# Sixteen-column offsets of TensorE operands: value weights moved, a copied operand dropped, dummy products put in front of long runs

## Chip, cores and metric

The kernel runs on one core of one Trainium2 chip. The metric is device time in microseconds (us) of one execution, the median of several. Engines are named as in the profile: PE is TensorE, DVE is VectorE, ACT is ScalarE, POOL is GpSimd, SP is the engine that issues most DMAs; PEld is the loading of PE's stationary operand.

## The reference

Two layers on 512 tokens of width 1024, in float32: first an HGRN2 mixer, then dilated attention, each followed by a gated feed-forward network (FFN). Only these parts matter here:

```python
def dilated_attention_mixer(u, cos, sin, w_in, w_out):
    proj = (u @ w_in).astype(jnp.float32).reshape(B, S, N_GROUPS, 3, ATT_HEADS, ATT_HEAD_DIM)
    ...
    for gi, (window, dilation) in enumerate(DILATED_GROUPS):
        q = apply_partial_rope(proj[:, :, gi, 0], cos, sin) * scale
        k = apply_partial_rope(proj[:, :, gi, 1], cos, sin)
        v = proj[:, :, gi, 2]
        o_g, lse_g = dilated_group_attention(q, k, v, window, dilation)
    ...

def swiglu_ffn(u, w_in, w_out):
    gate, up = jnp.split(u @ w_in, 2, axis=-1)
    return (jax.nn.silu(gate) * up) @ w_out
```

The FFN's inner width is 2816, that is 22 blocks of 128; attention has three groups of 8 heads of 128.

## The kernel before

**Products.** A float32 product is made of three products of the type float32r: each operand is cut into a high and a low part (`uh`, `ul` for the tokens, `hiq`, `loq` or `spare` for weights), and high by high, high by low and low by high are summed in a PSUM bank. A product (one `matmul`) has a stationary operand of 128 columns, which PE loads first, and a moving operand, here of 256 columns for nearly all that the change touches. The profile writes a product as `out<-moving,...` or `out<-stationary,...` with two tile names; which of the two moves is told below.

**Seven products for eight.** Where a block of weights is multiplied with all tokens, both are cut in quarters and the result is made from seven quarter products with sums of quarters (Strassen's scheme in Winograd's form). One quarter product is four slices of the contraction by three, so 12 products; a *group* below is such a run of 12 (for values, two groups of 12, one for each half of a PSUM bank).

**The FFN** (`seven_products`, products at line 964). Per inner block of 128 (called an iteration here) there are seven groups, 84 products: `B11` (tokens' first quarter), `T3`, `t2`, `B21`, `t1`, `T4`, `B22`. Layer 0 has 16 such iterations and layer 1 has 18; the first blocks of each layer (`PLAIN`) are done with products 512 columns wide at lines 577 to 579, just ahead. The moving operands are the tokens `uh`, `ul` and the sums of their quarters `th`, `tl`; stationary are the weights, in tiles that begin `R0` = 16 columns into their place. The weights of iteration i+1 are cut and summed by ACT, DVE and POOL while PE works on iteration i; the order of all this is written out by hand at the end of `seven_products`.

**The copied operand.** `B11` exists twice: as it lies, for the first iteration, and as a copy 144 columns further on (`uh[:, k, 144:400]`), for all later ones. `shift()` makes the copy once per layer, in place, in the middle of the first iteration: two casts on ACT for `uh`, two on DVE for `ul` (line 897).

**Attention's projections** (`products`, line 1982) are tasks of a planner (`Plan`): each task has an engine, a cost and its reads and writes; `run` tries several rules, keeps the order with the earliest end, and then writes the instructions in that order on every engine. Queries and keys of two groups are made by seven products (`sevens`): moving are the tokens (`apart`, `uh`, `th`, `tl`), stationary the weights, 16 columns into their place (`R0`). Queries and keys of the remaining group (`plain`) are 512 wide. Values of these two groups (`value_unit`) are made by seven products with the roles changed: here the weights move, `V0` = 32 columns into their place, and the tokens are stationary. One value unit has seven results of 24 products; the planner puts the four units into two long runs of two units (336 products) each. Softmax, rotary embedding and sums over values run between these, on the other engines and in short products on PE (lines 2248, 2273, 2321, 2342).

**Offsets.** All operand tiles begin in SBUF at a multiple of 128 bytes, 32 columns of four bytes. So the place of an operand's first column, in columns modulo 32, is 0 or 16 for everything here. Written as moving/stationary, the products of the kernel before are:

| products | moving/stationary | the two are |
|---|---|---|
| FFN, all groups but the copied `B11` | 0/16 | unequal |
| FFN, `B11` from the second iteration on (144 columns further) | 16/16 | equal |
| queries and keys by `sevens` | 0/16 | unequal |
| values (32 columns into their place) | 0/0 | equal |

Of the kernel before, what the change touches and what calls it, by code (L numbers as in the profile page):

```python
# [11 lines left out]
F32 = mybir.dt.float32  # L12
# [5 lines left out]
P = 128  # L18
# [15 lines left out]
MAGIC = 12582912.0  # L34
WHOLE = ("quarters", "half")

R0, V0 = 16, 32


class Stream:  # L40
# [100 lines left out]
class Plan:  # L141
# [3 lines left out]
    DRAIN = {"DVE": 0.12, "ACT": 0.12}  # L145

    def __init__(self):
        self.tasks, self.names, self.seq = [], {}, {}

    def add(self, eng, cost, fn=None, r=(), w=(), goal=None, late=None, urgent=False):  # L150

# [85 lines left out]
    def run(self):  # L237

        ts = self.tasks
        for t in ts:  # L240
            for d in t["deps"]:
                ts[d]["outs"].append(t["id"])
        due = [0.0] * len(ts)
        for t in reversed(ts):
            at = min([due[o] - self.after(t, ts[o]) for o in t["outs"]], default=1e9)
            if t["goal"] is not None:
                at = min(at, t["goal"] + t["cost"])
            due[t["id"]] = at - t["cost"]
        tries = (self.trial(due, *rule) for rule in itertools.product((1, 2, 3, 5), (0.1, 0.2, 0.3), (5.0, 8.0, 1e9), (0.3, 1.0)))
        end, done, start = min(tries, key=lambda r: r[0])  # L250
        for t in done:
            t["start"], t["due"] = start[t["id"]], due[t["id"]]
        for t in done:
            if t["fn"]:
                t["fn"](t["eng"])
        return done
# [36 lines left out]
def block_kernel(tc, x, c, positions, ada_w, ada_b, norm_g, hgrn_w_in, lower, hgrn_norm_g, hgrn_w_out,  # L293
# [8 lines left out]
    with ExitStack() as ctx:  # L302
# [579 lines left out]
        def seven_products(fs, mid, seeded, spare, th, tl):  # L882
# [5 lines left out]
            t_of = lambda i: [(th[:, i, k], tl[:, i, k]) for k in range(4)]  # L888
            B21, B22 = u_of(1, 0), u_of(1, 1)

            B11 = [u_of(0, 0), [(uh[:, k, 144:400], ul[:, k, 144:400]) for k in range(4)]]

            def shift():

                for a, b in ((112, 256), (0, 112)):
                    for copy, t in ((act.copy, uh), (dve.tensor_copy, ul)):
                        copy(t[:, 0:4, a + 144:b + 144], t[:, 0:4, a:b].bitcast(F32))
            t1, T3, T4, t2 = (t_of(i) for i in range(4))

            W = shared.rearrange("p a (b n) -> p (a b) n", b=2)  # L900
# [74 lines left out]
            with tc.manual_schedule(engines=ORDERED):  # L975
# [10 lines left out]
                for i in range(len(fs)):  # L986
                    more = i + 1 < len(fs)
                    R, Sm = places(i)
                    s = Sums(i)
                    run(s.first, R, 0, B11[i > 0], True)  # L990
                    run(s.both, Sm, 1024, T3, True)
                    if before:
                        gate_of(i - 1, before)
                    act.copy(s.u2, s.first)
                    if more:
                        r_lo(i + 1)
                        sum_a(i + 1)
                    if before:
                        value_of(i - 1, before)
                    run(s.u2, Sm, 0, t2, False)  # L1000
                    run(s.first, R, 1024, B21, False)
                    act.copy(W[:, 4 + i % 2], s.both)
                    act.copy(s.u4, s.u2)
                    if i == 0:
                        shift()
                    run(s.u4, Sm, 512, t1, False)
                    run(s.u2, R, 512, T4, False)
                    if more:
                        sum_b(i + 1)
# [604 lines left out]
        for p in range(4):  # L1614
# [11 lines left out]
            for k in range(2):  # L1626
# [5 lines left out]
                if k == 1:  # L1632
                    for i in range(2):
                        n = fl.n + i
# [338 lines left out]
        def split_place(first):  # L1973
            return plan.place("hl", 3, lambda: st.part_tiles(first))

        def products(cost, dst, key, terms, begin, reads):


            def go():
                todo = [p for t in terms() for p in t]  # L1980
                for i, (x, y) in enumerate(todo):
                    pe.matmul(dst(), x, y, start=begin and i == 0, stop=i == len(todo) - 1, skip_group_check=True)  # L1982
            of_units.append(len(plan.tasks))
            PE(cost, go, reads, [key])

        triple = lambda xh, xl, yh, yl: ((xh, yh), (xh, yl), (xl, yh))
        a_of = lambda r, c: [[a[:, r * 4 + k, c * 256:c * 256 + 256] for a in apart] for k in range(4)]
# [117 lines left out]
        def plain(g, hd):  # L2105
# [16 lines left out]
            def both():  # L2122
# [4 lines left out]
                def one(i, t):  # L2127
                    b = mm_of()
                    for part in range(4):
                        def terms(part=part):  # L2130
                            for kt in (2 * part, 2 * part + 1):
                                w = slice((i * KT + kt) * P, (i * KT + kt + 1) * P)
                                yield triple(p.t[0][:, w], p.t[1][:, w], apart[0][:, kt], apart[1][:, kt])
                        products(6 * 0.2275, lambda: b.t, b(), terms, part == 0, [p("h", i), p("l", i)])
                    scale = SCALE if i == 0 else 1.0
                    for hf in range(2):
                        o = i * 64 + hf * 32
# [12 lines left out]
        def value_unit(i, hf):  # L2150
# [46 lines left out]
            def run(tag, tile, o, us):  # L2197
                b, p = mm_of(tag), ps[tile]
                for n in range(2):
                    def terms(n=n):  # L2200
                        for kt in range(4):
                            w = slice(o * 1024 + kt * 256, o * 1024 + (kt + 1) * 256)
                            yield triple(*us(kt, n), p.t[0][:, w], p.t[1][:, w])
                    products(12 * 0.1165, lambda n=n: b.t[:, n * 256:(n + 1) * 256], b(), terms, n == 0, [p("h", o), p("l", o)])
                return b

            def add_to(out, one, b, f):
# [293 lines left out]
```

## Time and profile before

| | us |
|---|---|
| median of 3 executions (lowest, highest) | 1506.12 (1504.59, 1506.7) |
| the profiled execution | 1504.35 |
| its span | 1502.6 |
| PE busy in it | 1476.8 |
| DVE, ACT, POOL busy | 1095.8, 797.2, 191.3 |

The span is the time between the first and the last instruction; the profiled execution took 1.75 us more than it. PE's clock was granted in full (0.997 on average). A row of the view of groups reads: line, engine, operation, `out<-in` by tile names, shapes, count | busy time, mean duration in ns | idle time just before. A row of the timeline reads: start in us from the span's start, duration, engine, line, operation, names, shapes, count [idle time before it and what ended it]. Products overlap in PE's pipeline, so the duration of one (276 to 287 ns here) is longer than the distance from its start to that of the next; the distance is found from two start times and the number of products between them, and it is what a product costs.

### The profile page before, as it was taken

To read this page: it belongs to the slowest core of one execution; us is meant where nothing else is said; L and a number is where in the kernel's file an instruction comes from. 1 tells how busy PE (TensorE), PEld (TensorE's weight loads), DVE (VectorE), ACT (ScalarE), POOL (GpSimd) and SP (SyncE) were. 2 spreads that over 40 slices of the span, in tenths; PEclk is the share of its full clock that TensorE was granted. 3 is DMA by queue.
4 is the path that set the end of the run, shared out by engine and by line. 5 is a ranking of instruction groups with operands and counts; after the bars stand their busy time and mean duration, and the time that the engine had idled before them with its cause. 6 is when DMAs were issued, how large, how long until landed. Compare 5 with 4: busy or idle time off the path is not lost. (4 is left out here: it accounts for less than half of the span.)

```text
span 1502.6 us, 25061 instructions
## 1 busy us (share of the span) xinstructions
PE 1476.8 (98%) x9823; PEld 1323.5 (88%) x9823; DVE 1095.8 (73%) x1800; ACT 797.2 (53%) x1474; POOL 191.3 (13%) x172
## 2 busy tenths in 40 slices
PE   8999999999999999999999999999989999999998
PEld 6777788888999988788999999999978899999886
DVE  4587678487688885777798877888666978887533
ACT  4433343373455542267647878477875555555231
POOL 1011011031111100131001010001012211110100
PEclk9999999999999999999999999999999999999999
DMA  9654555124233346634344442345243333333531
GB/s 308 183 170 140 183 169 169 57 79 146 85 113 113 113 161 211 220 117 143 113 120 144 109 136 73 118 131 147 89 134 119 104 94 113 113 113 141 197 111 56
DMA packets 210151, 201.09 MB, mean 134 GB/s; under 512 B 8248, under 2 KB 167920, under 8 KB 209776
## 3 DMA queue, kind: packets, MB, share of 16 engines
q1 hardware_dynamic: 207056, 192.71, 41.3%
q10 hardware_dynamic: 1952, 6.65, 1.2%
q8 instruction: 77, 1.26, 0.4%
q0 software_dynamic: 1024, 0.13, 0.2%
q14 instruction: 42, 0.34, 0.1%
HBM read 192.31 MB, written 5.31 MB: 132 GB/s over the span
## 5 line engine op out<-in xcount | busy, mean ns | idle before, releaser
L90 ACT CAST hi<-raw 128x2048 fp32r<-128x2048 f32 x43 | 82.1, 1909 | 144.3 <-DMA raw<-in_ffn_w_out_dram 74.9
L91 DVE TENSOR_TENSOR lo<-raw,hi 128x2048 fp32r<-128x2048 f32 x43 | 103.7, 2413 | 65.7 <-ACT hi L90 65.6
L577 PE MATMUL ps_mm<-uh,hi 128*128 128x512 f32 (+1 forms) x400 | 145.6, 364 | 0.0
L578 PE MATMUL ps_mm<-ul,hi 128*128 128x512 f32 (+1 forms) x400 | 144.5, 361 | 1.1 <-DVE ul L677 1.1
L579 PE MATMUL ps_mm<-uh,lo 128*128 128x512 f32 (+1 forms) x400 | 143.9, 360 | 0.0
L1982 PE MATMUL ps_mm<-apart,hiq 128*128 128x256 f32 (+1 forms) x608 | 142.0, 326 | 0.1
L1982 PEld LDWEIGHTS ps_mm<-apart,hiq 128*128 128x128 f32 x608 | 100.0, 189 | 8.4 <-ACT xs L2096 0.3
L1982 PE MATMUL ps_mm<-apart,loq 128*128 128x256 f32 (+1 forms) x304 | 97.4, 321 | 0.4 <-DVE loq L2118 0.4
L964 PE MATMUL ps_mm<-tl,hiq 128*128 128x256 f32 x340 | 94.0, 276 | 0.0
L964 PE MATMUL ps_mm<-th,hiq 128*128 128x256 f32 x340 | 94.0, 276 | 0.0
L964 PE MATMUL ps_mm<-th,loq 128*128 128x256 f32 x340 | 94.0, 276 | 0.0
L955 DVE TENSOR_TENSOR loq<-raw,hiq 128x1024 fp32r<-128x1024 f32 x68 | 80.3, 1221 | 18.6 <-ACT hiq L951 18.6
L577 PEld LDWEIGHTS ps_mm<-uh,hi 128*128 128x128 f32 x400 | 75.2, 188 | 18.2 <-issue 6.7
L578 PEld LDWEIGHTS ps_mm<-ul,hi 128*128 128x128 f32 x400 | 75.4, 189 | 12.3 <-DVE ul L677 1.5
L579 PEld LDWEIGHTS ps_mm<-uh,lo 128*128 128x128 f32 x400 | 75.1, 188 | 12.4 <-issue 1.1
L578 PE MATMUL ps_mm<-lo,oh 128*128 128x512 f32 x208 | 81.5, 392 | 2.4 <-DVE lo L91 2.4
L935 POOL TENSOR_TENSOR raw<-raw 128x512 f32<-128x512 f32 x34 | 44.8, 1318 | 303.1 <-DVE spare L931 138.5
L577 PE MATMUL ps_mm<-hi,oh 128*128 128x512 f32 x208 | 81.5, 392 | 0.0
L951 ACT CAST hiq<-raw 128x1024 fp32r<-128x1024 f32 x68 | 68.0, 1047 | 18.7 <-DVE raw L939 17.1
L1982 PE MATMUL ps_mm<-uh,hiq 128*128 128x256 f32 x256 | 71.9, 281 | 0.0
L1982 PE MATMUL ps_mm<-uh,loq 128*128 128x256 f32 x256 | 71.3, 279 | 0.0
L1982 PE MATMUL ps_mm<-ul,hiq 128*128 128x256 f32 x256 | 71.3, 278 | 0.0
(479 smaller groups left out, 4632.8 us busy)
## 6 DMA issues: line engine op xcount, KB each, us to landing
raw<-in_ada_w_dram SPq DMA_DIRECT2D x40, 1024.0 KB, 5.1
raw<-in_ffn_w_in_dram SPq DMA_DIRECT2D x136, 256.0 KB, 4.1
raw<-in_ffn_w_out_dram SPq DMA_DIRECT2D x22, 1024.0 KB, 5.1
raw<-in_attn_w_in_dram SPq DMA_DIRECT2D x64, 256.0 KB, 4.6
raw<-in_hgrn_w_in_dram SPq DMA_DIRECT2D x12, 1024.0 KB, 5.3
raw<-in_attn_w_in_dram SPq DMA_DIRECT2D x12, 1024.0 KB, 5.2
raw<-in_ffn_w_in_dram SPq DMA_DIRECT2D x10, 1024.0 KB, 6.5
raw<-in_attn_w_in_dram SPq DMA_DIRECT2D x16, 512.0 KB, 4.6
```

The costliest lines, as they stand in the source:

```text
L90: self.nc.scalar.copy(hi, t)
L91: self.nc.vector.tensor_sub(lo, t, hi.bitcast(F32))
L577: pe.matmul(ps, ah, bh, start=start, stop=False, skip_group_check=part)
L578: pe.matmul(ps, ah, bl, start=False, stop=False, skip_group_check=part)
L579: pe.matmul(ps, al, bh, start=False, stop=stop, skip_group_check=part)
L935: pool.tensor_add(r[:, 2], r[:, 2], r[:, 0])
L951: act.copy(hi, src)
L955: dve.tensor_sub(lo, src, hi.bitcast(F32))
L964: pe.matmul(ps, w[x][:, a], us[kt][y], start=begin and kt + m == 0, stop=kt == 3 and m == 2, skip_group_check=True)
L1982: pe.matmul(dst(), x, y, start=begin and i == 0, stop=i == len(todo) - 1, skip_group_check=True)
```

## The change

Four things are changed.

`V0` becomes 48, so the values' moving weights begin 16 columns further on: values are now 16/0, unequal.

The copied `B11` and `shift()` go: every iteration of the FFN uses the operand as it lies, 0/16.

In the first iteration of each layer's FFN, between `B11` and `T3`, three dummy products are issued. They have the first stationary weights and, moving, `uh[:, 0, 16:272]`, that is 16/16, equal. They write the PSUM bank that `T3` starts anew just behind, so nothing of them is kept.

The planner gets a set `asides`. After the order is chosen, it walks along PE's tasks; a stretch of tasks that all make 256-wide projections is one run. In it, it takes the first task that starts a value result; if 12 tasks or more stand from there to the end of the run, three dummy products are issued ahead of that task, with its first stationary operand and moving weights 16 columns off (48 + 16 = 64, so 0/0, equal). The dummies have no cost in the plan, and the order of the tasks is not touched.

```diff
-R0, V0 = 16, 32
+R0, V0 = 16, 48
...
+        narrow = []
+        for t in [t for t in done if t["eng"] == "PE"] + [{}]:
+            if t.get("narrow"):
+                narrow.append(t)
+                continue
+            first = next((k for k, u in enumerate(narrow) if u["aside"]), len(narrow))
+            if len(narrow) - first >= 12:
+                self.asides.add(narrow[first]["id"])
+            narrow = []
...
-            B11 = [u_of(0, 0), [(uh[:, k, 144:400], ul[:, k, 144:400]) for k in range(4)]]
-
-            def shift():
-
-                for a, b in ((112, 256), (0, 112)):
-                    for copy, t in ((act.copy, uh), (dve.tensor_copy, ul)):
-                        copy(t[:, 0:4, a + 144:b + 144], t[:, 0:4, a:b].bitcast(F32))
+            B11 = u_of(0, 0)
...
-                    run(s.first, R, 0, B11[i > 0], True)
+                    run(s.first, R, 0, B11, True)
+                    if i == 0:
+                        for _ in range(3):
+                            pe.matmul(s.both, R[0][:, 0:P], uh[:, 0, 16:272], start=True, stop=True, skip_group_check=True)
                     run(s.both, Sm, 1024, T3, True)
...
-                    if i == 0:
-                        shift()
...
-        def products(cost, dst, key, terms, begin, reads):
-
+        def products(cost, dst, key, terms, begin, reads, aside=None, narrow=True):
+            me = len(plan.tasks)
 
             def go():
                 todo = [p for t in terms() for p in t]
+                for _ in range(3 if me in plan.asides else 0):
+                    pe.matmul(dst(), todo[0][0], aside(), start=True, stop=True, skip_group_check=True)
                 for i, (x, y) in enumerate(todo):
                     pe.matmul(dst(), x, y, start=begin and i == 0, stop=i == len(todo) - 1, skip_group_check=True)
-            of_units.append(len(plan.tasks))
+            of_units.append(me)
             PE(cost, go, reads, [key])
+            plan.tasks[me].update(narrow=narrow, aside=begin and aside is not None)
...
-                    products(12 * 0.1165, lambda n=n: b.t[:, n * 256:(n + 1) * 256], b(), terms, n == 0, [p("h", o), p("l", o)])
+                    products(12 * 0.1165, lambda n=n: b.t[:, n * 256:(n + 1) * 256], b(), terms, n == 0, [p("h", o), p("l", o)],
+                             lambda: p.t[0][:, o * 1024 + 16:o * 1024 + 272])
```

In the built program PE has 12 products more, in four places of three, and its order is otherwise the same. The first place is layer 0 of the FFN; on PE the seam between `B11` and `T3` in the first iteration was

```order
L964 MATMUL ps_a_3368<-uh,spare_3081 128x256
L964 MATMUL ps_a_3368<-ul,spare_3081 128x256
L964 MATMUL ps_a_3368<-uh,spare_3082 128x256
L964 MATMUL ps_a_3370<-th_3084,hiq_3374 128x256
L964 MATMUL ps_a_3370<-tl_3085,hiq_3374 128x256
```

and is now

```order
L967 MATMUL ps_a_3368<-uh,spare_3081 128x256
L967 MATMUL ps_a_3368<-ul,spare_3081 128x256
L967 MATMUL ps_a_3368<-uh,spare_3082 128x256
L996 MATMUL ps_a_3370<-uh,spare_3081 128x256 x3
L967 MATMUL ps_a_3370<-th_3084,hiq_3374 128x256
L967 MATMUL ps_a_3370<-tl_3085,hiq_3374 128x256
```

so the three dummies stand alone between the two groups; layer 1 has the same seam. The other two places are the long value runs. The first of them begins on PE behind the scores of a head (`qk`, line 2256 of the changed kernel), where now stands

```order
L2256 MATMUL ps_a_6475<-qk_6471,qk_6467 128x256 x2
L1986 MATMUL ps_mm_6662<-hiq_6577,apart_6291 128x256 x3
L1988 MATMUL ps_mm_6662<-hiq_6577,apart_6291 128x256
L1988 MATMUL ps_mm_6662<-loq_6578,apart_6291 128x256
L1988 MATMUL ps_mm_6662<-hiq_6577,apart_6292 128x256
```

with the three dummies ahead of the run's first product. In the second long run they stand ahead of the second value result (`ps_a_9082`), since the first result's 12 opening products are divided from the rest by a head's scores and sums, and a run that begins in the middle of a result gets its dummies at the next one.

On DVE the two casts of `shift()` are gone in each layer, and the sums for the second iteration's weights (line 942) come one place earlier. It was

```order
L931 TENSOR_TENSOR loq_3391<-raw_3191,hiq_3390 128x1536
L1053 TENSOR_TENSOR mid_3074<-ps_mm_3312,sg_3362 128x512
L897 CAST ul<-ul 128x4x144
L1053 TENSOR_TENSOR mid_3074<-ps_mm_3337,sg_3363 128x512
L897 CAST ul<-ul 128x4x112
L939 TENSOR_TENSOR raw_3191<-raw_3191 128x1024
L943 TENSOR_TENSOR raw_3191<-raw_3191 128x512
```

and is now

```order
L934 TENSOR_TENSOR loq_3391<-raw_3191,hiq_3390 128x1536
L942 TENSOR_TENSOR raw_3191<-raw_3191 128x1024
L1057 TENSOR_TENSOR mid_3074<-ps_mm_3312,sg_3362 128x512
L946 TENSOR_TENSOR raw_3191<-raw_3191 128x512
L1057 TENSOR_TENSOR mid_3074<-ps_mm_3337,sg_3363 128x512
```

ACT loses its two casts per layer without any other move; POOL and the DMA queues keep their order.

More of the change, by code (lines that the diff above doesn't have):

```diff
@@ L147, in __init__ @@
     def __init__(self):
-        self.tasks, self.names, self.seq = [], {}, {}
+        self.tasks, self.names, self.seq, self.asides = [], {}, {}, set()
     def add(self, eng, cost, fn=None, r=(), w=(), goal=None, late=None, urgent=False):
@@ L2133, in terms @@
                                 yield triple(p.t[0][:, w], p.t[1][:, w], apart[0][:, kt], apart[1][:, kt])
-                        products(6 * 0.2275, lambda: b.t, b(), terms, part == 0, [p("h", i), p("l", i)])
+                        products(6 * 0.2275, lambda: b.t, b(), terms, part == 0, [p("h", i), p("l", i)], narrow=False)
                     scale = SCALE if i == 0 else 1.0
```

## Prediction, made before the changed kernel ran

> **What bounds the kernel now.** I read the page first: PE is the bound almost everywhere, at full clock.
>
> ```profile
> span 1502.6 us, 25061 instructions
> PE 1476.8 (98%) x9823; PEld 1323.5 (88%) x9823; DVE 1095.8 (73%) x1800; ACT 797.2 (53%) x1474; POOL 191.3 (13%) x172
> ...
> PEclk9999999999999999999999999999999999999999
> ```
>
> So a nanosecond per product counts, and I looked for products of one shape that cost different amounts. PE's timeline around the FFN of layer 0 (rows at the seams of groups; the last two are from layer 1):
>
> ```profile
> 384.72 0.39 PE L579 MATMUL ps_mm<-uh,lo 128*128 128x512 f32 x1
> 384.95 0.28 PE L964 MATMUL ps_a<-uh,spare 128*128 128x256 f32 x1
> 386.36 0.28 PE L964 MATMUL ps_a<-th,hiq 128*128 128x256 f32 x1
> ...
> 394.84 0.28 PE L964 MATMUL ps_b<-uh,hiq 128*128 128x256 f32 x1
> 395.20 0.28 PE L964 MATMUL ps_b<-uh,hiq 128*128 128x256 f32 x1
> 396.28 0.29 PE L964 MATMUL ps_b<-th,hiq 128*128 128x256 f32 x1
> 396.63 0.28 PE L964 MATMUL ps_b<-th,hiq 128*128 128x256 f32 x1
> 397.65 0.28 PE L964 MATMUL ps_mm<-th,hiq 128*128 128x256 f32 x1
> 404.45 0.28 PE L964 MATMUL ps_a<-uh,spare 128*128 128x256 f32 x1
> 405.88 0.29 PE L964 MATMUL ps_a<-th,hiq 128*128 128x256 f32 x1
> ...
> 529.25 0.28 PE L964 MATMUL ps_b<-uh,hiq 128*128 128x256 f32 x1
> ...
> 1213.31 0.28 PE L964 MATMUL ps_b<-uh,hiq 128*128 128x256 f32 x1
> 1366.92 0.28 PE L964 MATMUL ps_b<-uh,hiq 128*128 128x256 f32 x1
> ```
>
> From 386.36 to 394.84 stand 72 unequal products (moving/stationary 0/16): 8.48/72 = 117.8 ns each. The second iteration begins with 12 equal ones (16/16, the copied `B11`), 1.44 us or 120 ns each. Three more products (396.28 to 396.63, 117 ns) and then 60 unequal ones, 397.65 to 404.45, take 113.3 ns. So the unequal products have two speeds, 117.8 (*slow*) and 113.3 (*quick*), and what stood between them was a stretch of equal products. Each later iteration repeats it: 1.43 us for its 12 equal products (119), the rest quick; thirteen iterations take 529.25 - 404.45 = 124.80, 9.600 each. Groups in the first iteration and in a quick stretch of the second tell the speeds by duration too:
>
> ```profile
> L964 PE MATMUL ps_mm<-th,hiq 128*128 128x256 f32 x8 | 2.2, 281 | 0.0
> ...
> L964 PE MATMUL ps_mm<-th,hiq 128*128 128x256 f32 x12 | 3.3, 276 | 0.0
> ```
>
> Then attention: queries and keys (rows 1 to 6), the value runs (the others).
>
> ```profile
> 777.58 0.28 PE L1982 MATMUL ps_mm<-uh,hiq 128*128 128x256 f32 x1
> 784.64 0.39 PE L1982 MATMUL ps_mm<-apart,hiq 128*128 128x512 f32 x1
> 798.54 0.28 PE L1982 MATMUL ps_mm<-uh,hiq 128*128 128x256 f32 x1
> 807.02 0.27 PE L2248 MATMUL ps_a<-qk,qk 128*128 128x128 f32 x1
> 809.93 0.28 PE L1982 MATMUL ps_mm<-uh,hiq 128*128 128x256 f32 x1
> 818.09 0.27 PE L2321 MATMUL ps_a<-ident,h 128*128 128x128 f32 x1
> ...
> 733.35 0.47 PE L1982 MATMUL ps_mm<-hiq,apart 128*128 128x256 f32 x1
> 736.42 0.28 PE L1982 MATMUL ps_a<-hiq,uh 128*128 128x256 f32 x1
> 773.85 0.28 PE L1982 MATMUL ps_mm<-apart,hiq 128*128 128x256 f32 x1
> ...
> 940.97 0.28 PE L1982 MATMUL ps_a<-hiq,uh 128*128 128x256 f32 x1
> 975.15 0.28 PE L1982 MATMUL ps_mm<-hiq,apart 128*128 128x256 f32 x1
> ```
>
> 777.58 to 784.64 are 60 unequal products at 117.7, 798.54 to 807.02 another 72 at 117.8; behind a head's scores (line 2248), 809.93 to 818.09, 72 of the same kind at 113.3. Either speed lasts through seven groups and all their tiles: it is a state of PE that something else sets. The equal values are never quick: 736.42 to 773.85 are 312 products at 120.0, 940.97 to 975.15 are 288 at 118.7.
>
> **FFN.** If the three equal dummies set the quick state, and it lasts, an iteration costs 84 x 0.1133 = 9.52 instead of 9.60. The first iteration had 9.89; it now has 12 x 0.1178 + 3 x 0.120 + 72 x 0.1133 + 0.02 for settling = 9.95, so +0.06. The second goes from 9.61 to 9.52, the 14 behind it save 0.08 each: layer 0 gains 0.09 + 1.12 - 0.06 = 1.15. Layer 1 runs (1366.92 - 1213.31)/16 = 9.60 too, with 17 iterations behind its first: 1.36 - 0.06 = 1.30. Together **-2.45**.
>
> That three products do the work of twelve is not shown. What I have is the first three of the twelve, 394.84 to 395.20: 120 ns each, already the pace of the whole stretch, so they are in their own rhythm at once; and that the change of speed comes two or three products after the offset turns back. I take it that the turn from equal to unequal sets the state. If it does not, every unequal product of the FFN is slow, the rival below.
>
> **Values.** From 0/0 to 16/0, behind dummies of 0/0: the mirror image of the FFN, 16 columns displaced. No product 16/0 is in the trace. Its bounds are 113.3 and 120.0; I take 113.3, by the FFN's seam, the only equal-to-unequal turn there in which the moving operand's offset changes. The first run: 336 x 6.7 ns = 2.25, less 3 x 0.12 + 0.02 = 0.38: -1.87. The second, behind its dummies: 312 x 5.4 = 1.68 - 0.38 = -1.30. Together -3.17.
>
> Who comes late then is DVE, which prepares all weights (first row: a window with the busy time of PE, PEld, DVE, ACT and POOL in it, the clock, and the share and GB/s of DMA; then DVE's timeline, and a row of PE's waits: us, count, mean):
>
> ```profile
> 751.00:785.00 34.00, 34.00 (x286) 33.83 (x285) 31.10 (x46) 14.51 (x21) 0.58 (x1) 1.00 0.40 114
> ...
> 751.02 0.69 DVE L2224 SCALAR_TENSOR_TENSOR V<-V,ps_mm 128x512 f32<-128x512 f32 x1 [1.58 <-PE ps_mm L1982]
> 782.42 0.42 DVE L2091 TENSOR_TENSOR qk<-xs,ps_mm 128x256 f32<-128x256 f32 x1 [0.80 <-ACT xs L2096]
> 784.38 1.23 DVE L2118 TENSOR_TENSOR loq<-raw,hiq 128x1024 fp32r<-128x1024 f32 x1
> ...
> PE ps_mm L1982 <- DVE loq L2118: 0.4, 1, 0.4
> ```
>
> From 751.00 to 785.00 DVE is busy 31.10 of 34.00 us, and PE waits 0.4 for its cut at 784.38. At 751.02 PE is (751.02 - 733.35)/0.120 = 147 products into the run, so earlier by 147 x 6.7 ns - 0.38 = 0.60; DVE shifts with it, and another 0.80 can come out of its wait at 782.42 (for ACT, which waits for PE): 1.40 against PE's 1.87. I charge **+0.4**, with 0 to 1.3 as bounds. In the second run DVE waits for others, and I charge nothing.
>
> What the first run's end does to queries and keys behind it is open too. 773.85 to 807.02 holds 168 slow unequal products: quick, they give -0.76, but the scores at 807.02 came between slow and quick, and may then do the reverse to the 84 behind (+0.38). I take 0 of -0.8 to +0.4.
>
> **Copies.** The view of line 897:
>
> ```profile
> L897 DVE CAST ul<-ul x4: 394/427/875, 382.2 to 1204.9; 128x576 fp32r<-128x576 f32 x2, 128x448 fp32r<-128x448 f32 x2
> L897 ACT CAST uh<-uh x4: 567/622/677, 389.7 to 1208.8; 128x576 fp32r<-128x576 f32 x2, 128x448 fp32r<-128x448 f32 x2
> ```
>
> Eight casts, about 2.5 us on ACT and 2 on DVE, in the first iterations; nobody waits for them there, PE's 84 products run without a gap. Value: 0.
>
> **Sum.** -2.45 - 3.17 + 0.4 = -5.2 on the profiled execution's 1504.35, so 1499.1. The median of three, 1506.12, is 1.8 above it: **1500.9**.
>
> The Trainium skill speaks against all of it. Its page "TensorE: Matmul & The Clock Gate" (section "Back-to-back issue gap") gives a spacing from the moving width alone, 109.2 ns for 256 columns, and says under "Step-by-step: what each phase is for" that moving and stationary operands have independent read ports. By that, dummies are pure cost, an estimated 12 x 109.2 = 1.3 us. The trace disagrees: 113.3, 117.8 and 120.0 ns for one width.
>
> **Rivals.**
>
> *The quick state is not set by three, or does not last.* Each iteration of the FFN now needs the state from its layer's only dummies, where before it was renewed by 12 equal products every 9.6 us. Without it 84 x 0.1178 = 9.895: layer 0 loses 15 x 0.295 + 0.36 = 4.8, layer 1 17 x 0.295 + 0.36 = 5.4, together +10.2; with the values at -2.8 that is +7.4, 1513.5, and 1516 if these stay slow too. It decides as soon as the state is lost within the first two thirds of a layer. For it: an unequal stretch never ran quick for longer than 84 products. Against: no quick stretch in the FFN falls back, nor has it stalls that could disturb it. Chance 0.22.
>
> *The values do not become quick*, since 16/0 behaves otherwise or the scores ahead of the run win. Slow at 117.8 they save 336 x 2.2 + 312 x 0.9 ns = 1.02 and cost 0.72 of dummies: with the FFN -2.75, 1503.4. Chance 0.19.
>
> *Offsets do nothing*, and the speeds have another cause, such as which iteration it is. Then the trace's rows stay and 12 dummies at 0.113 are added: +1.4, 1507.5. Against it is the timing of the seams. Chance 0.06.
>
> **How the numbers follow.** The likeliest, 0.53, is 1500.9; its own range, with a wait of DVE from 0 to 1.3, queries and keys from -0.8 to +0.4 and the runs' scatter of 1 us, is 1499 to 1503. The range takes in the second and third rival and the nearest of the first's partial losses: 1498.5 to 1509. 0.2% is 3.0 us, about what a measurement of this kernel can tell from no change. Faster by more: the likeliest and a part of the second rival, 0.60. Within: most of the second and half of the third, 0.17. Slower: the first and the rest, 0.23.
>
> **What would show it.** In line 967's groups of the changed kernel: 281 ns only in the first 12 products of each layer, 276 after; iterations of 9.52. In line 1988's value groups: 276 instead of 282 to 288. PE's wait for DVE near 785 grown from 0.4 to about 1. If the first `T3` group behind the dummies still shows 281, the forecast is wrong by some 10 us; if a later iteration turns to 281, the state does not last.

## The result, and the profile after

| | before, us | changed, us | ratio (95% interval) |
|---|---|---|---|
| first comparison, medians of 15 and 15 executions | 1504.23 | 1499.83 (1493.97 to 1503.32) | 0.9968 (0.9957 to 0.9979) |
| the same kernel again, 17 and 6 executions | 1503.39 | 1498.41 (1495.14 to 1502.71) | 0.9957 (0.9941 to 0.9973) |

The change makes the kernel faster by 0.32%, 4.8 us of 1504 (3.2 to 6.5), and by 6.5 us (4.1 to 8.9) the second time. 1500.9 us and -5.2 were predicted. The profiled execution took 1503.32 us and is the slowest of its 15, so the span below differs from that before by 1.0 us only; what it lost is told at the end of this section.

The head of the page of the changed kernel (1502.6 us and 1476.8 us of PE before):

```profile
span 1501.6 us, 25079 instructions
PE 1472.6 (98%) x9835; PEld 1317.9 (88%) x9835; DVE 1091.9 (73%) x1796; ACT 793.4 (53%) x1470; POOL 191.8 (13%) x172
```

PE's timeline at the FFN of layer 0 (the last two rows are of layer 1):

```profile
384.45 0.28 PE L967 MATMUL ps_a<-uh,spare 128*128 128x256 f32 x1
385.86 0.52 PE L996 MATMUL ps_a<-uh,spare 128*128 128x256 f32 x3
386.22 0.29 PE L967 MATMUL ps_a<-th,hiq 128*128 128x256 f32 x1
386.93 0.28 PE L967 MATMUL ps_a<-th,hiq 128*128 128x256 f32 x1
394.41 0.28 PE L967 MATMUL ps_b<-uh,hiq 128*128 128x256 f32 x1
...
527.69 0.28 PE L967 MATMUL ps_b<-uh,hiq 128*128 128x256 f32 x1
...
1213.64 0.28 PE L967 MATMUL ps_b<-uh,hiq 128*128 128x256 f32 x1
1365.96 0.28 PE L967 MATMUL ps_b<-uh,hiq 128*128 128x256 f32 x1
```

The dummies of line 996 take 0.36 us. The six products behind them still settle (386.22 to 386.93, 118 ns each); from there 66 products reach 394.41 at 7.48/66 = 113.3 ns. The fourteen iterations from 394.41 to 527.69 take 133.28/14 = 9.520 us each, the sixteen of layer 1 152.32/16 = 9.520 too: no iteration falls back. The view of groups for the first iteration tells it by duration (mean ns behind the comma):

```profile
L967 PE MATMUL ps_mm<-th,hiq 128*128 128x256 f32 x8 | 2.2, 276 | 0.0
```

Those `ps_mm` products were at 281 before. The value runs, in PE's timeline:

```profile
731.93 0.28 PE L1988 MATMUL ps_mm<-hiq,apart 128*128 128x256 f32 x1
734.66 0.28 PE L1988 MATMUL ps_a<-hiq,uh 128*128 128x256 f32 x1
770.02 0.28 PE L1988 MATMUL ps_mm<-apart,hiq 128*128 128x256 f32 x1
...
944.68 0.28 PE L1988 MATMUL ps_mm<-hiq,apart 128*128 128x256 f32 x1
977.32 0.39 PE L1988 MATMUL ps_mm<-apart,hiq 128*128 128x512 f32 x1
```

734.66 to 770.02 are 312 products at 113.3 ns (120.0 before), 944.68 to 977.32 are 288 at 113.3 (118.7 before).

PE's products without the dummies are the same 9823 in the same order in both kernels, so the time between the starts of two of them can be compared. This table, worked out from the start times, gives the differences to the kernel before in us for the stretches that matter (named by their times in the kernel before), for the changed kernel's two profiles and for those experiments that keep the order:

| stretch | changed | again | FFN alone | values alone | no dummies | unequal | one dummy |
|---|---|---|---|---|---|---|---|
| FFN of layer 0 (384.9 to 539.3) | -1.15 | -1.15 | -1.15 | 0.00 | +4.39 | +4.74 | -1.39 |
| first value run and its dummies (700 to 773.9) | -1.87 | -1.87 | 0.00 | -1.87 | -0.74 | -0.39 | -1.28 |
| second value run (935.4 to 978) | -1.33 | -1.33 | 0.00 | -1.33 | -0.33 | +0.02 | -1.57 |
| FFN of layer 1 (1203.3 to 1377.2) | -1.32 | -1.32 | -1.32 | 0.00 | +4.97 | +5.32 | +5.09 |
| sum of these four | -5.67 | -5.67 | -2.47 | -3.20 | +8.29 | +9.69 | +0.85 |
| waits behind the first run (773.9 to 784.6) | +1.07 | 0.00 | 0.00 | +0.40 | 0.00 | 0.00 | 0.00 |
| the head behind it (784.6 to 819.6) | +2.95 | +1.39 | -0.01 | +0.23 | -0.01 | +1.32 | 0.00 |
| last heads' sums (1093.8 to 1170) | +1.77 | +0.73 | -3.41 | +1.57 | -3.43 | -3.45 | -2.89 |
| time by the ratio of medians | -4.8 | -6.5 | -3.8 | -1.1 | +9.0 | +10.1 | +1.1 |

The first four rows follow the products and repeat to 0.01 us where a kernel was profiled twice. The others don't. Views of the changed kernel show what PE waited for between 770 and 822 us; first its waits (us, count, longest):

```profile
PE ps_mm L1988 <- ACT xs L2103: 1.8, 1, 1.8
PE ps_a L2281 <- ACT h L2337: 1.1, 1, 1.1
PE ps_mm L1988 <- DVE loq L2125: 0.5, 1, 0.5
PE ps_mm L1988 <- ACT hiq L2124: 0.4, 1, 0.4
PE ps_mm L1988 <- ACT ps_mm L2078: 0.4, 1, 0.4
```

The last three, 1.3 us, are the cuts of weights and what hangs on them. Only the 0.5 us for `loq` is PE's wait for DVE. It was 0.4 before, and it is 0.5 in all three profiles with quick values; about 1 was predicted. The other two are waits for ACT, which the profile of the same kernel again doesn't show; ACT had itself waited for DVE shortly before each (0.20 and 1.16 us), so DVE may stand behind them, but no run shows it. The second wait, 1.1 us (0.4 before), is at the scores that end the next stretch. The first one, 1.8 us, is something else; POOL's timeline and then a row of DVE's:

```profile
805.17 0.55 POOL L2295 DMA_DIRECT2D scr<-so  x1 [55.31 <-ACT h L2293]
808.71 0.77 POOL L2297 DMA_DIRECT2D so<-scr  x1 [2.99 <-DMA scr<-so]
```

```profile
814.16 0.17 DVE L2306 TENSOR_TENSOR wM<-so 128x8 f32<-128x8 f32 x1 [3.28 <-DMA so<-scr]
```

A head's sums go through DRAM and back in two small copies. The first took 3.54 us to the issue of the second, the second another 5.4 until DVE could start. In the kernel before the rows are

```profile
807.67 0.54 POOL L2287 DMA_DIRECT2D scr<-so  x1 [55.83 <-ACT h L2285]
809.63 0.76 POOL L2289 DMA_DIRECT2D so<-scr  x1 [1.42 <-DMA scr<-so]
```

with 1.96 us for the first, and nobody waited. In the kernels with the values alone and with no dummies it is 1.96 again, in the one with unequal dummies, whose values are not quick, 3.08. So these 3 us are no price of the values' speed. Whether they are one of the dummies is open: the first copy took 3.08 to 3.54 us in the five profiles of kernels with twelve dummies (one of them with a new order), and 1.95 to 2.12 in the eight of kernels with none, fewer or many more. The last of these chains, near 1110 us, makes PE wait 0.8 to 1.4 us in some profiles (FFN alone, no dummies, unequal dummies, one dummy) and 2.7 to 3.8 in others (before, changed twice, values alone).

### The profile page after: what moved, and what is told of

Its sections match the earlier page's. It is cut to its first block, busy times and chain, and to the rows that moved or that the text cites. A ratio compares the mean times of both kernels' runs of the same rounds, so it can differ in the third digit from the quotient of the medians.

```text
span 1501.6 us, 25079 instructions
## 1 busy us (share of the span) xinstructions
PE 1472.6 (98%) x9835; PEld 1317.9 (88%) x9835; DVE 1091.9 (73%) x1796; ACT 793.4 (53%) x1470; POOL 191.8 (13%) x172
```

## Experiments

All comparisons are against the kernel before, on the same chip. "Dummies" are the products that the change adds; *slow* is 117.8 ns and *quick* 113.3 ns per unequal product, as in the prediction.

**The FFN's half alone.**

```diff
-R0, V0 = 16, 48
+R0, V0 = 16, 32
...
-                for _ in range(3 if me in plan.asides else 0):
+                for _ in range(0):
```

> Only the FFN half of the change: V0 is 32 again and the value runs have no dummies; B11 is not copied and three equal dummies stand in the first iteration of each layer. My theory (equal dummies set a quick state that lasts): from the second T3 group of a layer on every FFN group at 113.3 ns per product, an iteration 9.52 us instead of 9.60, the values as before at 120.0 and 118.7 ns; -2.45 us against the kernel before. Rival (the gain of the whole change came from the values alone, the FFN being within noise): 0.

Measured: ratio 0.9975 (0.9963 to 0.9987), -3.8 us (-5.6 to -2.0); both layers' iterations at 9.52 us, -2.47 us in the four stretches. The theory holds at these places, and the rival (0) is out.

**The values' half alone**: the FFN of the kernel before, with `shift()` and the copied `B11`, in the changed kernel, and no dummies there.

```diff
...
-                    run(s.first, R, 0, B11, True)
-                    if i == 0:
-                        for _ in range(3):
-                            pe.matmul(s.both, R[0][:, 0:P], uh[:, 0, 16:272], start=True, stop=True, skip_group_check=True)
+                    run(s.first, R, 0, B11[i > 0], True)
...
```

> Only the values' half: the FFN as in the kernel before (copied B11, shift, no dummies there), V0 = 48 and three equal dummies ahead of the two value runs. My theory: 336 and 312 value products at 113.3 ns, -3.2 us before waits; of the first run's 1.9 us a part comes back as PE's waits for DVE and ACT right behind it (770 to 820 us), 0.4 expected, at most 1.3 if only the queue of cuts is late: -2.8, at least -1.9. Rival (what lies behind the first value run is bound by DVE and ACT, so that its gain is given back whole): -1.3, that of the second run alone.

Measured: 0.9993 (0.9981 to 1.0005), -1.1 us (-2.9 to +0.8). The time alone can't tell the two theories apart. The rows can: the runs give -1.87 and -1.33, and the two stretches behind the first give back 0.40 and 0.23, so 2.57 stays where the rival has 1.3. The profiled execution, with 1507.23 us the slowest of its 12, lost its time elsewhere: 2.35 us ahead of 384.9 us and 1.55 between 539.3 and 700, where the kernels do the same work, and 1.57 at the last heads' sums.

**No dummies**, and **dummies with unequal offsets**.

```diff
-                    if i == 0:
-                        for _ in range(3):
-                            pe.matmul(s.both, R[0][:, 0:P], uh[:, 0, 16:272], start=True, stop=True, skip_group_check=True)
...
-                for _ in range(3 if me in plan.asides else 0):
+                for _ in range(0):
```

> The whole change without any of its twelve dummies: V0 = 48, no copied B11. My theory: nothing sets the state, so every FFN product stays at 117.8 ns in both layers (9.90 us an iteration), +10.7 us from the FFN (34 x 84 x 4.5 ns less the copy's own 1.4 us of slow start is in it), and the values run at 117.8 ns with the state that the scores leave, -1.0: together +8 to +10. Rival (the quick state comes by itself behind the first iteration, or from the unequal offsets): FFN quick from the second iteration, -3 to -5 in all.

```diff
-                            pe.matmul(s.both, R[0][:, 0:P], uh[:, 0, 16:272], start=True, stop=True, skip_group_check=True)
+                            pe.matmul(s.both, R[0][:, 0:P], uh[:, 0, 0:256], start=True, stop=True, skip_group_check=True)
...
-                             lambda: p.t[0][:, o * 1024 + 16:o * 1024 + 272])
+                             lambda: p.t[0][:, o * 1024:o * 1024 + 256])
```

> The whole change, the twelve dummies at their places, but with moving operands that begin where the products' own begin: 0/16 in the FFN and 16/0 ahead of the values, unequal. My theory (the equal offsets do it): as without dummies, 117.8 ns in the whole FFN, +9 to +11 us. Rival (any dummies or the pause do it, or writing the bank twice): as the change, 113.3 ns, -4 to -5.

Measured: 1.0060 (1.0043 to 1.0078), +9.0 us, without dummies, and 1.0067 (1.0051 to 1.0084), +10.1, with unequal ones. PE's timeline without dummies, layer 0:

```profile
387.44 0.28 PE L967 MATMUL ps_a<-th,hiq 128*128 128x256 f32 x1
395.92 0.28 PE L967 MATMUL ps_b<-uh,hiq 128*128 128x256 f32 x1
534.42 0.28 PE L967 MATMUL ps_b<-uh,hiq 128*128 128x256 f32 x1
```

Fourteen iterations from 395.92 to 534.42 take 9.893 us each, 117.8 ns per product to the last one. Without dummies the two FFN layers lose 9.36 us (10.7 were expected). So the quick state neither comes by itself nor by three products more; the offset of the dummies' moving operand, 16 columns, is worth 15 us of the kernel's time (from +10.1 to -4.8).

**Fewer dummies**, another number at each place.

```diff
...
-                        for _ in range(3):
+                        for _ in range(1 if len(fs) == 16 else 2):
...
-                for _ in range(3 if me in plan.asides else 0):
+                for _ in range(1 + plan.asides.index(me) if me in plan.asides else 0):
```

> The change with fewer dummies, another number at each of the four places: one in the FFN of layer 0, two in layer 1, one ahead of the first value run, two ahead of the second. If the turn from equal to unequal sets the state, one is enough: every place runs at 113.3 ns behind it (FFN iterations of 9.52 us, value groups of 276 ns). Rival (a stretch of three or more equal products is needed, as PE comes into another rhythm only with the third): 117.8 ns behind a single dummy, and perhaps behind two; an FFN layer then takes 9.90 us an iteration.

Measured (one execution): 1498.25 us. All four places became quick. But the first value run, behind one dummy, fell back in the middle; PE's timeline:

```profile
762.71 0.28 PE L1988 MATMUL ps_mm<-hiq,uh 128*128 128x256 f32 x1
762.83 0.34 PE L1988 MATMUL ps_mm<-loq,uh 128*128 128x256 f32 x1
763.00 0.28 PE L1988 MATMUL ps_mm<-hiq,ul 128*128 128x256 f32 x1
```

One product came 60 ns late (762.83 to 763.00), and the rest of the run, 94 products, is at 117.8 ns. A stall can end the state, then; it happened behind three dummies too, as a run below shows.

**Other turns**: three dummies at each place with the other pairs of offsets.

```diff
...
-                            pe.matmul(s.both, R[0][:, 0:P], uh[:, 0, 16:272], start=True, stop=True, skip_group_check=True)
+                            pe.matmul(s.both, uh[:, 0, 0:P], uh[:, 0, 0:256] if len(fs) == 16 else uh[:, 0, 16:272], start=True, stop=True, skip_group_check=True)
...
-                    pe.matmul(dst(), todo[0][0], aside(), start=True, stop=True, skip_group_check=True)
+                    pe.matmul(dst(), apart[0][:, 0, 16:144], aside(plan.asides.index(me)), start=True, stop=True, skip_group_check=True)
...
-                             lambda: p.t[0][:, o * 1024 + 16:o * 1024 + 272])
+                             lambda k: p.t[0][:, o * 1024 + 16 * k:o * 1024 + 16 * k + 256])
```

> Three dummies at each place, with other offsets (moving/stationary), so that another turn stands in front of the run: 0/0 ahead of the FFN of layer 0 (equal; the moving offset stays, the stationary one changes), 16/0 ahead of layer 1 (unequal; both change), 16/16 ahead of the first value run (equal; only the stationary one changes), 0/16 ahead of the second (unequal; both change). My theory (what sets the quick state is a change of the moving operand's offset while the stationary one's stays): slow, 117.8 ns, behind all four. Rival A (any equal products set it): quick behind 0/0 in layer 0 and behind 16/16 in the first value run, slow at the other two. Rival B (any change of the moving offset sets it): quick in layer 1 and in the second value run, slow at the other two.

Measured (one execution): 1512.75 us. Slow in both layers and in the first value run, quick in the second. PE's timeline at the first run's start and end, then at the second's:

```profile
737.10 0.28 PE L1988 MATMUL ps_mm<-hiq,apart 128*128 128x256 f32 x1
776.68 0.40 PE L1988 MATMUL ps_mm<-apart,hiq 128*128 128x256 f32 x2
...
947.41 0.28 PE L1988 MATMUL ps_a<-hiq,uh 128*128 128x256 f32 x1
980.07 0.28 PE L1988 MATMUL ps_mm<-hiq,apart 128*128 128x256 f32 x1
```

39.58/336 = 117.8 ns and 32.66/288 = 113.4 ns. Behind three unequal dummies 0/16 a run 16/0 was quick: mine misses the last place, rival A three of the four, rival B layer 1. Equal products aren't needed, and aren't enough.

**The changed kernel again**, and **with the planner told the new speed**.

> The changed kernel itself, once more. If the 2.95 us that the stretch behind the first value run (784.6 to 819.6 us of the kernel before) lost in its first profile came from the time of two small DMAs through DRAM, which differs from execution to execution, it is another number here, 0 to 1.5 us; if the value run's gain is what makes this wait, it is again about 3. The stretch 773.9 to 784.6, which waits for the cuts of weights, should lose 0.4 to 1.1 again. Time against the kernel before: -0.2 to -0.4%.

Measured: the second row of the result's table. The two stretches behind the first value run lost 0.00 and 1.39 us, against 1.07 and 2.95 in the first profile. The 0.00 misses the 0.4 to 1.1 expected of the cuts of weights. The 1.39 is another number, as expected of the copies through DRAM, and the kernel with the values alone, 0.23, says the same more clearly. But the wait of 3.8 us for the last heads' copies came again.

```diff
-                    products(12 * 0.1165, lambda n=n: b.t[:, n * 256:(n + 1) * 256], b(), terms, n == 0, [p("h", o), p("l", o)],
+                    products(12 * 0.1133, lambda n=n: b.t[:, n * 256:(n + 1) * 256], b(), terms, n == 0, [p("h", o), p("l", o)],
```

> The change, and the planner is told that a value task of 12 products costs 12 x 0.1133 us instead of 12 x 0.1165, so that it orders the work behind the runs by their new speed. If PE's new waits behind the first value run (0.4 to 1.1 us at 773.9 to 784.6) come from an order made for a slower run, they go and the time falls by up to 1 us against the changed kernel; if DVE simply is too late there (31 of 34 us busy), they stay, 0; the order of a whole layer is made anew, so +-1 either way elsewhere.

Measured: 0.9976 (0.9963 to 0.9990), -3.6 us, against 0.9957 (0.9941 to 0.9973) for the changed kernel beside it: no gain shown. PE still waits 0.5 us for `loq` and 0.3 for `xs` behind the run. The new order also made PE wait inside the first value run; PE's timeline at that wait and at the run's end:

```profile
759.39 0.38 PE L1988 MATMUL ps_mm<-loq,uh 128*128 128x256 f32 x1 [0.40 <-DVE loq L2170]
759.62 0.28 PE L1988 MATMUL ps_mm<-hiq,ul 128*128 128x256 f32 x1
770.69 0.40 PE L1988 MATMUL ps_mm<-apart,hiq 128*128 128x256 f32 x2
```

Ahead of it the run was quick; behind it the last 94 products take 11.07/94 = 117.8 ns. So three dummies don't protect a run from a stall.

**A map of the turns**: other dummies in 33 of the 34 iterations. `SEQ` has, for each iteration, stretches (m, q, n): n dummies whose moving operand begins at 16m and whose stationary one at 16q.

```diff
-                    if i == 0:
-                        for _ in range(3):
-                            pe.matmul(s.both, R[0][:, 0:P], uh[:, 0, 16:272], start=True, stop=True, skip_group_check=True)
+                    for m, q, n in SEQ[i if len(fs) == 16 else 16 + i]:
+                        for _ in range(n):
+                            pe.matmul(s.both, R[0][:, 0:P] if q else uh[:, 0, 0:P], uh[:, 0, 16:272] if m else uh[:, 0, 0:256], start=True, stop=True, skip_group_check=True)
```

> A map of the turns: in each of the 34 FFN iterations other dummies stand between B11 and T3 (0/0, 16/0 or 16/16, in stretches of 1, 2, 3 or 12, also two stretches one behind the other), and the 72 unequal products 0/16 behind them tell the state. What is left from the earlier runs: 16/16 in front sets quick, from one product on; 0/0 and 16/0 in front of a slow stretch leave it slow; the last run's 0/16 dummies made a value run 16/0 quick, against my theory. Theory 2 (the last stretch alone decides: 16/16 gives quick, 0/0 and 16/0 give slow, whatever the state and the count before): quick in the iterations whose dummies end with 16/16, slow in those that end with 0/0 or 16/0. Rival (a turn shifts a phase, so that the state before and the count of dummies count too): 0/0 or 16/0 from the quick state leave it quick in some, or one dummy acts otherwise than two or twelve. Time: some 300 dummies, about +37 us, and the slow iterations.

Measured (one execution): 1529.70 us, with 226 dummies in the FFN instead of the 300 reckoned with. Two places with one dummy 16/16 behind a slow stretch, in PE's timeline (dummy, first product behind it, first of the next iteration, 72 products later):

```profile
452.04 0.28 PE L997 MATMUL ps_a<-uh,spare 128*128 128x256 f32 x1
452.16 0.28 PE L968 MATMUL ps_a<-th,hiq 128*128 128x256 f32 x1
460.63 0.28 PE L968 MATMUL ps_b<-uh,hiq 128*128 128x256 f32 x1
...
472.06 0.28 PE L997 MATMUL ps_a<-uh,spare 128*128 128x256 f32 x1
472.18 0.28 PE L968 MATMUL ps_a<-th,hiq 128*128 128x256 f32 x1
480.36 0.28 PE L968 MATMUL ps_b<-uh,hiq 128*128 128x256 f32 x1
```

8.47/72 = 117.6 ns in the first, 8.18/72 = 113.6 in the second: the same dummy, the same pace before (117.8), another state behind. All places with one kind of dummies, these two among them, from the start times (state before and behind as the mean spacing of the 0/16 products):

| dummies | behind a slow stretch | behind a quick stretch |
|---|---|---|
| 16/16, one | quick in 2 of 7 | quick in 4 of 4 |
| 16/16, two | | slow, 1 |
| 16/16, twelve | quick, 1 | |
| 0/0, one or two | slow, 3 (the first of layer 1 among them) | |
| 0/0, twelve | | slow, 1 |
| 16/0, one | | slow, 1 |
| 16/0, two | slow, 2 | |
| 16/0, three | quick, 1 | slow, 1 |
| 16/0, twelve (their own pace) | quick, 1 (117.9) | slow, 1 (113.5) |

The other places have two kinds of dummies one behind the other. The rival holds: the state before and the count matter, and unequal 16/0 can set the state as well as undo it. The second theory (the last stretch alone decides) falls.

**How sure three are.** The same kernel, with twelve 0/0 in every other iteration and 16/16 in the next.

```diff
-SEQ = [[], [(1, 1, 12)], [(0, 0, 12)], [(1, 0, 12)], [(1, 1, 1)],
...
+SEQ = [[(0, 0, 12)], [(1, 1, 3)], [(0, 0, 12)], [(1, 1, 3)],
...
```

> How sure three dummies are. In every other FFN iteration twelve dummies 0/0 set the slow state (they did so in all three places of the map), and in the next one stand 16/16: three dummies ten times, two dummies three times, six twice, and four times three dummies behind a stretch that is quick already. If three set the state whatever came before, all fourteen places with three run at 113.3 ns behind them. Rival (a phase that a dummy may or may not shift, as with one dummy, which set it in 2 of 7 places behind a slow stretch): some of the ten stay at 117.8 ns, and the change has its time by a lucky place; two dummies then differ from three. Time: about 150 dummies, +18 us, and 15 slow iterations, +4 us, against the changed kernel.

Measured (one execution): 1532.90 us, with 240 dummies in the FFN instead of the 150 reckoned with, and 25 slow iterations instead of 15. A reset is the stretch of twelve 0/0 and the slow products behind it. Three behind a reset in layer 0, two behind a reset in layer 1, and three behind the slow stretch that three had left:

```profile
397.30 0.52 PE L997 MATMUL ps_b<-uh,hiq 128*128 128x256 f32 x3
397.66 0.28 PE L968 MATMUL ps_b<-th,hiq 128*128 128x256 f32 x1
406.14 0.28 PE L968 MATMUL ps_a<-uh,spare 128*128 128x256 f32 x1
...
1228.58 0.40 PE L997 MATMUL ps_b<-uh,hiq 128*128 128x256 f32 x2
1228.81 0.28 PE L968 MATMUL ps_b<-th,hiq 128*128 128x256 f32 x1
1236.98 0.28 PE L968 MATMUL ps_a<-uh,spare 128*128 128x256 f32 x1
...
1345.29 0.52 PE L997 MATMUL ps_a<-uh,spare 128*128 128x256 f32 x3
1345.64 0.29 PE L968 MATMUL ps_a<-th,hiq 128*128 128x256 f32 x1
1353.82 0.28 PE L968 MATMUL ps_b<-uh,hiq 128*128 128x256 f32 x1
```

117.8, 113.5 and 113.6 ns over the 72 products. Three behind a reset set the state in 0 of 10 places, two in 3 of 3, six in 2 of 2; three more behind a slow stretch that three had left, in 2 of 2, and behind a quick one it stayed quick in 2 of 2. The theory that three set it whatever came before falls, and it falls in one direction every time: this is a count that does or doesn't fit what stands before, not chance. The products ahead of the three ran at 117.8 ns where they failed and where they succeeded, so the pace doesn't tell the whole state. In the changed kernel, behind layers that begin slow, three fit in all ten FFN places that were profiled (the changed kernel twice, the FFN alone, the two kernels with another planned order) and in all fourteen at the values.

**One dummy at each place.**

```diff
-                        for _ in range(3):
+                        for _ in range(1):
...
-                for _ in range(3 if me in plan.asides else 0):
+                for _ in range(1 if me in plan.asides else 0):
```

> The change with one dummy instead of three at each of the four places. By the run with counts one is enough; 8 products less at 0.12 us are -0.96 us in PE's rows, and -0.9 us of the time against the changed kernel, about -0.4% against the kernel before. Rival (a single dummy holds less well: a value run fell back to 117.8 ns behind a stall of 60 ns in that run): 0 to +0.5 against the changed kernel.

Measured: 1.0007 (0.9994 to 1.0020), 1504.27 us: the whole gain is gone. PE's timeline of layer 1 (the dummy, the product behind it, the starts of the second and the last iteration):

```profile
1198.30 0.28 PE L996 MATMUL ps_a<-uh,spare 128*128 128x256 f32 x1
1198.42 0.28 PE L967 MATMUL ps_a<-th,hiq 128*128 128x256 f32 x1
1206.90 0.28 PE L967 MATMUL ps_b<-uh,hiq 128*128 128x256 f32 x1
1365.19 0.28 PE L967 MATMUL ps_b<-uh,hiq 128*128 128x256 f32 x1
```

158.29/16 = 9.893 us an iteration: this layer stayed slow to its end, +5.09 us; layer 0 became quick. The first value run fell back behind a stall here too. Neither side expected as much: what one dummy risks is a whole layer.

**The copies through DRAM issued by ACT**, since their waits hide 3 to 5 us.

```diff
-                POOL(0.85, lambda: pool.dma_start(scr[hd, 0].rearrange("(t p) s -> p t s", p=P), so.t[:, 0, 1]), [so("N", t) for t in range(NT)],
+                ACT(0.1, lambda: act.dma_start(scr[hd, 0].rearrange("(t p) s -> p t s", p=P), so.t[:, 0, 1]), [so("N", t) for t in range(NT)],
...
```

> The change, and the four small copies through DRAM that a head's sums take (scr, so) are issued by ACT instead of POOL. In all profiles so far PE waits 0.8 or 2.7 to 3.8 us for the last of these chains, whichever the kernel. If the software queue's time is what makes these waits and the spread between executions (10 us of the changed kernel), waits at that place of about 1 us and a time 1 to 3 us below the changed kernel; if any DMA through DRAM takes that long, the same waits, and ACT stalls behind the second copy: 0 to +3 us. The planner makes a new order for it, worth another +-1.

Measured: 1.0098 (1.0081 to 1.0115), +14.7 us, more than either side expected. ACT's waits between 700 and 1130 us:

```profile
ACT hiq L2169 <- DMA scr<-so: 11.9, 2, 6.3
ACT qk L2148 <- DMA scr<-so: 8.4, 1, 8.4
```

The second copy's issue waits for the first copy in ACT's queue, and the cuts of weights stand behind it. The planner's whole order is another too, so the +14.7 isn't all of that, and what the software queue's time costs stays open. The first value run, behind three dummies, was held up four times here, with 0.32 to 1.83 us from one start to the next, and was quick again behind each: a stall can also leave the state.

## Why the prediction was right, and where its reason failed

**FFN, -2.45.** Measured -2.47 in the rows, layer by layer -1.15 and -1.32 (predicted -1.15 and -1.30), and the FFN alone gave -3.8 us (-5.6 to -2.0). The price of the first iteration, the 9.52 us of all others, and the loss without the state (+4.39 and +4.97 against predicted 4.8 and 5.4, which had 0.36 each of dummies in them) came out as worked out.

**Values, -3.17.** -1.87 and -1.33 measured, -1.87 and -1.30 predicted: a run 16/0 can be quick, at the same 113.3 ns. Left without dummies the values were at 117.8, as the second rival had it.

**The step that failed** is the reason given for both: "I take it that the turn from equal to unequal sets the state". Three equal products behind a reset left the FFN slow in ten of ten places; two set it in three of three; three unequal 0/16 set a value run quick, and one dummy at the same turn left a whole layer at 9.893 us an iteration. What stands in its place: PE's state behind a turn depends on the offsets of the dummies, on their number and on the state before. That looks like a phase between two streams which each dummy moves by some step, but this is argued from the counts and not shown; which step, and between what, stays open. So the first rival ("not set by three, or does not last") has a real mechanism. It didn't come about here because the places of the change are entered in a state for which three fit, every time they were profiled. The forecast's time was right, its confidence in three products was not earned by the row it was taken from (the pace of the first three of twelve): that three was a number that fits was luck.

**Does it last?** Over 16 and 18 iterations, in every profile that got it, as forecast. The FFN has no stalls behind its dummies. The value runs show that a stall can end it: 60 ns late was enough behind one dummy, a wait of 0.40 us ended it behind three, and four hold-ups of another kernel's run, the longest 1.83 us from start to start, did not.

**DVE's wait, +0.4 within 0 to 1.3.** The stretch behind the first value run gave back 1.07, 0.00 and 0.40 us in three profiles. The bounds held, the term behind them did not: PE's wait for DVE near 785 grew from 0.4 to 0.5 us in all three, not to about 1, and what was lost beyond that went to waits for ACT. And one thing was missed: the state of the queries and keys there is changed by the stalls themselves (in the first profile the products behind the stall at 774 run at 113 ns up to the next change of shape), so the term "-0.8 to +0.4" and this one are not independent.

**Copies, 0.** Layer 0's -1.15 is what the products alone give; nothing is left over for them.

**The sum** of the first four stretches is -5.67, and waits of 0 to 4 us behind it differ between profiles; the two ratios, -4.8 and -6.5 us, lie around it. For every kernel of the table but one the sum of the four lies within the interval of the measured time; for the values alone (-3.20 against -2.9 to +0.8) it does with the waits behind the run.

**The rival that offsets do nothing**, and the rule of a spacing by width alone, would have made the change cost time; the no-dummies and unequal kernels, 9 and 10 us slower with the same widths, rule both out here. The section "Back-to-back issue gap" of the Trainium skill's page "TensorE: Matmul & The Clock Gate", which the prediction cites for 109.2 ns, calls its formula the gap of an isolated matmul and says that in a stream the weight load shares in the spacing, so the figure is not the page's forecast for these streams, in which 113.3 to 120.0 ns were measured.

## What to carry to other kernels

Look at the mean duration of products of one shape, stretch by stretch: 276 against 281 ns, or 113.3 against 117.8 ns from start to start, was worth 15 us here, and no wait, busy share or clock shows it. If some products in front of a long run set its speed, count how many and test them behind the state in which they will stand: two, three and six were not the same, and one cost a layer its gain. Then look for stalls inside the run, since one of them can undo the speed. A gain of 0.3% is to be read from the starts of the same products in two profiles, since waits behind small copies through DRAM move the total by 3 to 5 us in either direction.

## What the hardware showed that was not expected

Products of one shape with unequal offsets have two steady speeds, 113.3 and 117.8 ns, each kept over 1300 products, and go from one to the other at a turn of offsets or at a stall. Twelve products 16/0 in the FFN ran at the speed of the stretch 0/16 ahead of them (117.9 behind slow, 113.5 behind quick, once each), and the 0/16 products behind them had the other speed. The first of the two copies told of above, 4 KB to DRAM, took 1.95 to 2.12 us until the next issue in eight profiles and 3.08 to 3.54 in five; what decides between the two wasn't found. The same copy for the other heads of the changed kernel took from 2.08 to 6.72 us in one profile.
